# The order of the seven products in the feed-forward stages of a one-core trunk kernel

## The chip, the cores and the metric

The program runs on one core of a Trainium2 chip. The metric is the device time of one execution in microseconds (us); lower is better. Before the change it is 2337.01 us, the median of three runs (2335.78 to 2339.98).

## What is computed

The reference is a two-layer diffusion trunk: 1024 latent tokens of width 1024, and a context of 256 tokens. Each layer normalises and modulates the tokens, mixes them (Fourier and state-space groups in layer 0, gating and pooling groups in layer 1), projects, and adds the result. Then each layer runs the part that matters here, a squared-ReLU feed-forward network of hidden width 4096:

```
lat = lat + g_f * (square(relu(h @ w1)) @ w2)       # h: 1024 x 1024, w1: 1024 x 4096, w2: 4096 x 1024
```

Everything is float32. A float32 product is made on TensorE from a rounded part ("hi") and a remainder ("lo") of both operands, in three matmuls: hi*hi, hi*lo and lo*hi (`mm3`).

## The kernel before

**Seven products in place of eight.** Both halves of the feed-forward network are multiplied by a fast 2x2 block scheme. A product P1 to P7 multiplies one combination of weight blocks with one combination of activation blocks (a *set*). The table `PRODUCTS` (line 259) gives for each product its weight tile, its set, and one of three accumulators in PSUM: `a`, `b` or `d`. P1, P6, P7 and P4 all add onto accumulator `a`, one after another; P5 and P3 share `d`; P2 has `b` to itself. So the running value in `a` must be read out after P1 before P6 may write, after P6 before P7 may write, and after P7 before P4 may write.

**Stages.** `ffn` (line 1535) runs 16 stages per layer, here numbered 0 to 15. Stages 0 to 7 make the hidden activations ("up"), two quads (pairs of column tiles) in each, stages 8 to 15 multiply them by `w2` ("down"), two quads in each except stage 15, which has one. A stage runs its seven products one after another. `product` (line 1521) issues for each quad 4 x 3 = 12 matmuls of 128x128 by 128x512. With two quads a product is 24 matmuls: quad 0, then quad 1. Six PSUM banks (`psg`) serve as accumulators: three per quad.

**Reading the accumulators.** In an up stage (`up_step`, line 1556) P1, P5 and P6 are copied from PSUM by ScalarE (line 1586), P2, P7 and P3 are added to one of these copies by VectorE (line 1588), and P4 goes through a ReLU on ScalarE (line 1590). After P2, P7 and P3 ScalarE also does a ReLU (1595) and a square (1564) over both quads. In a down stage (`down_step`, line 1615) VectorE reads all seven (`add_to`, line 1548): each adds the accumulator times a gain onto a tile of `lat`. The first use of a `lat` tile waits for its load (`need`, line 1609, DMA at line 501).

**Weights.** `Weights` (line 267) loads the blocks, forms the sums s1, s2, s3 (`sum`, line 286) and splits each into hi (ScalarE, line 489) and lo (VectorE, line 490). `split` works in the order in which the products use the weights. s4 = w12 - s2 is formed by VectorE (line 295) right after w12 was split. All weights rotate through 14 tiles, so a split often waits for a product to release a tile.

**Sets.** A finished set of the up stages goes to DRAM (`r_d`, DMA on POOL's queue, line 1561) and is loaded for the down stages one product at a time (`load_set`, line 1551, DMA on SP's queue, line 1476), into the place of a set that has been used for the last time, and is then split (`late`, `split_set`).

**Other work beside.** In layer 0 the feed-forward stages from stage 2 on also carry the modulation vectors of the next layer: `ada_steps` (line 646) loads 256 KB pieces (SP, line 654) and VectorE accumulates them (line 658).

**What sets the order.** Each engine executes its own queue in order. The framework places the instructions of the program into the queues ahead of time, by priority and by its own estimate of when each is ready; a split may stand a product or two earlier than in the program text. The order cannot change at run time. Stage 0 has an order of its own, `FIRST` (line 262: P1, P2, P5, P6, P7, P3, P4), which the change leaves alone; there the first product of stage 1 stands between P1 and P2. All other stages use `ORDER` (line 261).

The loops around the change, cut to their core:

```
for s, p in enumerate(w.order):     # ffn, line 1665
    run(p)                          # the product, its reads, puts or loads of sets
    ...
    w.step(s)                       # splits the weight used three products on
    nxt.step(s - 7)                 # loads, sums and splits for the next stage
```

Of the kernel before, what the change touches and what calls it, by code (L numbers as in the profile page):

```python
# [176 lines left out]
class FfnNorm:  # L177
# [44 lines left out]
    def second(self):  # L222
# [28 lines left out]
        for j in range(2):  # L251
# [6 lines left out]

PRODUCTS = {"p1": ("w11", "b11", "a"), "p2": ("w12", "b21", "b"), "p3": ("s4", "b22", "d"), "p4": ("w22", "t4", "a"),
            "p5": ("s1", "t1", "d"), "p6": ("s2", "t2", "a"), "p7": ("s3", "t3", "a")}  # L260
ORDER = ["p1", "p5", "p6", "p2", "p7", "p3", "p4"]
FIRST = ["p1", "p2", "p5", "p6", "p7", "p3", "p4"]
SETS = ["b11", "t1", "t2", "b21", "t3", "b22", "t4", "b12"]
SETPOOL = {"b11": "C", "t1": "A", "t2": "A", "b21": "A", "b22": "A", "t3": "B", "t4": "B", "b12": "B"}


# [188 lines left out]
class Trunk:  # L455
# [257 lines left out]
    def layer0_mixer(self):  # L713
# [8 lines left out]
        self.col_d = dp.tile([32, 3, L], F32R, name="col_d")  # L722
        self.r_d = dp.tile([4, len(SETS), P, 4 * HALF], F32, name="r_d")
        self.hb_d = dp.tile([2, NCH, P, 512], F32, name="hb_d")
# [774 lines left out]
    def up_weights(self, layer, n):  # L1499
# [3 lines left out]
        def block(q):  # L1503
            return lambda i, j: w[j * 512:(j + 1) * 512, (4 * n + 2 * q + i) * P:(4 * n + 2 * q + i + 1) * P].rearrange(
                "(k p) c -> p k c", p=P)

        return Weights(self, [block(q) for q in range(2)], ORDER if n else FIRST)

# [26 lines left out]
    def ffn(self, layer, norm, extra, after, first, last):  # L1535
# [15 lines left out]
        def load_set(chunk, p):  # L1551
            src = self.r_d[chunk, SETS.index(p)].rearrange("p (k t) -> p k t", t=HALF)
            sets[p] = self.from_scratch(SETPOOL[p], "r", src)
            late.append(sets[p])

        def up_step(n, w, last_pair, start=None):
# [3 lines left out]
            def put(name):  # L1560
                nc.gpsimd.dma_start(self.r_d[chunk, SETS.index(name)][:, q0 * HALF:(q0 + 2) * HALF], self.flat(tmp[name]))

# [52 lines left out]
        def down_step(chunk, quads, w, final):  # L1615
            banks = {}
            hits = {"p1": (0, 0), "p5": (1, 1), "p6": (0, 1), "p2": (0, 0), "p7": (1, 1), "p3": (0, 1), "p4": (1, 0)}

            def run(p):
                i, hf = hits[p]  # L1620
                for n, q in enumerate(quads):
                    ct = 2 * q + i
                    ps = self.product(banks, w, p, n, sets)
                    need(q, hf)
                    add_to(ct, hf, ps)
                    if final and p in ("p2", "p7", "p3", "p4"):
                        for b, (h, sl) in enumerate(after.blocks):
                            if h == hf:
                                after(ct, b, lat[ct][hf][:, sl])
                if chunk < 3 and quads[-1] == 3:  # L1630
                    load_set(chunk + 1, PRODUCTS[p][1])

            return run
# [13 lines left out]
        for chunk in range(4):  # L1647
            for quads in ((0, 1), (2, 3)) if chunk < 3 else ((0, 1), (2,)):
                w = Weights(self, [self.down_block(layer, chunk, q) for q in quads], ORDER)
                stages.append((w, down_step(chunk, quads, w, chunk == 3)))  # L1650
# [296 lines left out]
```

## Time and profile before

| | |
|---|---|
| median of three runs | 2337.01 us |
| the profiled execution | 2340.41 us, of which span 2338.3 us |
| mean granted TensorE clock | 0.995 of full speed |
| matmul (PE) busy | 2287.6 us, 98% of the span |
| VectorE (DVE) busy | 1595.7 us, 68% |
| ScalarE (ACT) busy | 986.1 us, 42% |
| GpSimd (POOL) busy | 178.5 us, 8% |

The rows come from one profiled execution. In the rows PE is TensorE's matmuls, PEld its weight loads, and SPq and POOLq are the DMA queues of SyncE and GpSimd. L1586 is line 1586 of the kernel. The time between the profiled execution's own time and its span, 2.1 us, lies around the first and last instruction. A matmul's duration in the rows is that of a pipelined instruction; the distance between two starts is what it costs.

### The profile page before, as it was taken

To read this page: it belongs to the slowest core of one execution; us is meant where nothing else is said; L and a number is where in the kernel's file an instruction comes from. 1 tells how busy PE (TensorE), PEld (TensorE's weight loads), DVE (VectorE), ACT (ScalarE), POOL (GpSimd) and SP (SyncE) were. 2 spreads that over 40 slices of the span, in tenths; PEclk is the share of its full clock that TensorE was granted. 3 is DMA by queue.
4 is the path that set the end of the run, shared out by engine and by line. 5 is a ranking of instruction groups with operands and counts; after the bars stand their busy time and mean duration, and the time that the engine had idled before them with its cause. 6 is when DMAs were issued, how large, how long until landed. Compare 5 with 4: busy or idle time off the path is not lost. (4 is left out here: it accounts for less than half of the span.)

```text
span 2338.3 us, 27846 instructions
## 1 busy us (share of the span) xinstructions
PE 2287.6 (98%) x10445; PEld 1840.6 (79%) x10445; DVE 1595.7 (68%) x2100; ACT 986.1 (42%) x1385; POOL 178.5 (8%) x303
## 2 busy tenths in 40 slices
PE   7999999999999999999999999999989999999998
PEld 2787777777877888878888887888868888788887
DVE  4777778757378676778877639642496555887785
ACT  3656664443136454633433322231255554543242
POOL 0003002111000101100001000000010101000000
PEclk9999999999999999999999999999999999999999
DMA  8545567648514656763554225752124536754422
GB/s 306 174 127 160 163 218 247 206 158 303 164 50 167 207 199 222 275 234 123 189 173 132 70 72 176 230 202 104 55 98 157 178 126 222 273 189 171 135 88 111
DMA packets 305169, 400.52 MB, mean 171 GB/s; under 512 B 22063, under 2 KB 222379, under 8 KB 297611
## 3 DMA queue, kind: packets, MB, share of 16 engines
q1 hardware_dynamic: 257952, 297.75, 38.8%
q0 software_dynamic: 30656, 91.78, 10.5%
q10 hardware_dynamic: 16427, 9.22, 1.3%
q8 instruction: 82, 1.34, 0.2%
q14 instruction: 52, 0.43, 0.1%
HBM read 282.27 MB, written 116.39 MB: 170 GB/s over the span
## 5 line engine op out<-in xcount | busy, mean ns | idle before, releaser
L478 PE MATMUL psg<-hhi,whi 128*128 128x512 f32 x1088 | 429.0, 395 | 9.7 <-ACT hhi L489 4.6
L478 PE MATMUL psg<-hlo,whi 128*128 128x512 f32 x1088 | 427.3, 393 | 2.9 <-DVE hlo L490 2.9
L478 PE MATMUL psg<-hhi,wlo 128*128 128x512 f32 x1088 | 424.9, 391 | 0.0
L478 PE MATMUL psg<-rhi,whi 128*128 128x512 f32 (+1 forms) x920 | 356.3, 387 | 5.6 <-DVE lat L1548 5.6
L478 PE MATMUL psg<-rlo,whi 128*128 128x512 f32 (+1 forms) x920 | 355.4, 386 | 0.0
L478 PE MATMUL psg<-rhi,wlo 128*128 128x512 f32 (+1 forms) x920 | 355.1, 386 | 0.0
L478 PEld LDWEIGHTS psg<-hhi,whi 128*128 128x128 f32 x1088 | 205.4, 189 | 56.6 <-ACT hhi L489 7.1
L489 ACT CAST whi<-ww 128x1024 fp32r<-128x1024 f32 (+1 forms) x128 | 131.2, 1025 | 278.4 <-DVE wlo L490 229.3
L478 PEld LDWEIGHTS psg<-hlo,whi 128*128 128x128 f32 x1088 | 205.3, 189 | 48.3 <-DVE hlo L490 5.5
L478 PEld LDWEIGHTS psg<-hhi,wlo 128*128 128x128 f32 x1088 | 205.4, 189 | 43.7 <-issue 1.0
L490 DVE TENSOR_TENSOR wlo<-ww,whi 128x1024 fp32r<-128x1024 f32 (+1 forms) x128 | 152.0, 1187 | 99.0 <-PE psg L478 89.5
L1548 DVE SCALAR_TENSOR_TENSOR lat<-psg,ada,lat 128x512 f32<-128x512 f32 (+1 forms) x220 | 162.7, 741 | 72.1 <-PE psg L478 54.4
L478 PEld LDWEIGHTS psg<-rhi,whi 128*128 128x128 f32 x920 | 173.2, 188 | 41.6 <-issue 5.6
L478 PEld LDWEIGHTS psg<-rlo,whi 128*128 128x128 f32 x920 | 173.2, 188 | 34.9 <-issue 0.2
L478 PEld LDWEIGHTS psg<-rhi,wlo 128*128 128x128 f32 x920 | 173.1, 188 | 34.5
L478 PE MATMUL psg<-h,whi 128*128 128x512 f32 (+1 forms) x672 | 196.1, 373 | 4.2 <-DVE h L509 3.4
L489 ACT CAST whi<-ws 128x1024 fp32r<-128x1024 f32 (+1 forms) x96 | 98.1, 1024 | 170.9 <-PE psg L478 89.7
L478 PE MATMUL psg<-yhi,whi 128*128 128x512 f32 x384 | 151.9, 396 | 2.2 <-ACT nss L133 1.8
L478 PE MATMUL psg<-yhi,wlo 128*128 128x512 f32 x384 | 150.3, 392 | 0.0
L478 PE MATMUL psg<-ylo,whi 128*128 128x512 f32 x384 | 149.8, 391 | 0.0
L490 DVE TENSOR_TENSOR wlo<-ws,whi 128x1024 fp32r<-128x1024 f32 (+1 forms) x96 | 113.9, 1186 | 51.5 <-PE psg L478 45.5
L489 ACT CAST rhi<-rlo 128x1024 fp32r<-128x1024 f32 x116 | 116.0, 1049 | 70.9 <-PE psg L478 46.6
(298 smaller groups left out, 3574.8 us busy)
## 6 DMA issues: line engine op xcount, KB each, us to landing
rlo<-r_d SPq DMA_DIRECT2D x58, 1024.0 KB, 6.8
ww<-in_ffn_w_dram SPq DMA_DIRECT2D x190, 256.0 KB, 5.2
r_d<-rt POOLq DMA_DIRECT2D x64, 512.0 KB, 6.5
araw<-in_ada_w_dram SPq DMA_DIRECT2D x56, 512.0 KB, 5.0
r_d<-uc POOLq DMA_DIRECT2D x36, 512.0 KB, 2.9
lat<-lat_d SPq DMA_DIRECT2D x32, 512.0 KB, 9.2
ws<-in_ffn_w_dram SPq DMA_DIRECT2D x62, 256.0 KB, 3.3
wraw<-in_ev_w_in_dram SPq DMA_DIRECT2D x24, 512.0 KB, 6.7
```

The source lines that it names most:

```text
L478: self.nc.tensor.matmul(out, lhsT=lhsT, rhs=rhs, start=start, stop=stop, skip_group_check=onto)
L489: self.nc.scalar.copy(hi, x)
L490: self.nc.vector.tensor_tensor(lo, x, hi.bitcast(F32), ALU.subtract)
L1548: nc.vector.scalar_tensor_tensor(lt, ps, g(ct), lt, ALU.mult, ALU.add)
```

## The change

Two products change places in `ORDER`, and the same two sets in `SETS`:

```diff
-ORDER = ["p1", "p5", "p6", "p2", "p7", "p3", "p4"]
+ORDER = ["p1", "p5", "p2", "p6", "p7", "p3", "p4"]
 FIRST = ["p1", "p2", "p5", "p6", "p7", "p3", "p4"]
-SETS = ["b11", "t1", "t2", "b21", "t3", "b22", "t4", "b12"]
+SETS = ["b11", "t1", "b21", "t2", "t3", "b22", "t4", "b12"]
```

In the 15 stages of each layer that use `ORDER`, P2 now comes third and P6 fourth. With them move: the reads of their accumulators, the split of w12 (now ahead of s2's), the forming of s4, the ReLU, square and put of P2's result, and in the loading stages the loads of the sets b21 (now third) and t2 (now fourth). `SETS` only names the place of each set in `r_d`. The number of instructions of every kind stays the same.

## Rows read from the trace of the kernel before

**Rows 1.** The page's first part: busy time, share of the span, instructions.

```profile
PE 2287.6 (98%) x10445; PEld 1840.6 (79%) x10445; DVE 1595.7 (68%) x2100; ACT 986.1 (42%) x1385; POOL 178.5 (8%) x303
```

**Rows 2.** The waits of PE: engine, waited for, us in total, times, longest.

```profile
PE psg L478 <- DVE lat L1548: 5.6, 3, 3.2
...
PE psg L478 <- ACT uc L1586: 2.0, 2, 1.0
```

**Rows 3.** Timeline, ACT, layer 1 stage 5: start, us, instruction, count, [idle before <-releaser].

```profile
1907.25 0.59 ACT L1586 COPY uc<-psg 128x512 f32<-128x512 f32 x1 [0.56 <-PE psg L478]
1909.97 0.59 ACT L1586 COPY uc<-psg 128x512 f32<-128x512 f32 x1 [2.13 <-PE psg L478]
...
1917.46 1.05 ACT L1595 ACTIVATE uc<-uc 128x1024 f32<-128x1024 f32 x1
1918.55 1.06 ACT L1564 ACTIVATE uc<-uc 128x1024 f32<-128x1024 f32 x1
```

**Rows 4.** Timeline, DVE, the same stage, the read of P2's second quad.

```profile
1916.39 0.68 DVE L1588 TENSOR_TENSOR uc<-psg,uc 128x512 f32<-128x512 f32 x1
```

**Rows 5.** Timeline, ACT, layer 1 stage 0, copies after P6.

```profile
1727.78 1.56 ACT L1586 COPY uc<-psg 128x512 f32<-128x512 f32 x3 [0.77 <-PE psg L478]
```

**Rows 6.** Timeline, PE, layer 1 stage 0, the first matmul of P7.

```profile
1728.42 0.50 PE L478 MATMUL psg<-hhi,whi 128*128 128x512 f32 x1 [1.04 <-ACT uc L1586]
```

**Rows 7.** Timeline, PE, stage 8: first matmuls of P6 (layer 0, then layer 1 twice).

```profile
1006.86 0.77 PE L478 MATMUL psg<-rhi,whi 128*128 128x512 f32 x1 [3.19 <-DVE lat L1548]
...
2020.12 0.47 PE L478 MATMUL psg<-rhi,whi 128*128 128x512 f32 x1 [1.39 <-DVE lat L1548]
...
2024.07 0.50 PE L478 MATMUL psg<-rhi,whi 128*128 128x512 f32 x1 [0.98 <-DVE lat L1548]
```

**Rows 8.** Timeline, DVE, layer 0 stage 8, reads of accumulators.

```profile
1005.96 0.75 DVE L1548 SCALAR_TENSOR_TENSOR lat<-psg,ada,lat 128x512 f32<-128x512 f32 x1 [6.83 <-DMA lat<-lat_d]
...
1013.57 1.40 DVE L1548 SCALAR_TENSOR_TENSOR lat<-psg,ada,lat 128x512 f32<-128x512 f32 x2
...
1017.16 0.74 DVE L1548 SCALAR_TENSOR_TENSOR lat<-psg,ada,lat 128x512 f32<-128x512 f32 x1
...
1020.09 0.74 DVE L1548 SCALAR_TENSOR_TENSOR lat<-psg,ada,lat 128x512 f32<-128x512 f32 x1
```

**Rows 9.** Timeline, DVE, layer 1 stage 8, the seventh read.

```profile
2034.51 0.75 DVE L1548 SCALAR_TENSOR_TENSOR lat<-psg,ada,lat 128x512 f32<-128x512 f32 x1
```

**Rows 10.** Busy time by window: stretch, length, busy (count) per engine, PEclk, DMA, GB/s.

```profile
1006.00:1010.00 4.00, 3.14 (x8) 2.56 (x9) 3.00 (x4) 0.00 (x0) 0.53 (x1) 0.57 1.07 375
```

**Rows 11.** Timeline, DVE, layer 0, stages 2, 4 and 6.

```profile
772.28 1.53 DVE L658 SCALAR_TENSOR_TENSOR aacc<-araw,silu,aacc 128x512 f32<-128x512 f32 x2 [6.37 <-DMA araw<-in_ada_w_dram]
...
781.22 1.21 DVE L490 TENSOR_TENSOR wlo<-ww,whi 128x1024 fp32r<-128x1024 f32 x1
...
857.01 1.22 DVE L490 TENSOR_TENSOR wlo<-ww,whi 128x1024 fp32r<-128x1024 f32 x1
...
935.46 1.22 DVE L490 TENSOR_TENSOR wlo<-ww,whi 128x1024 fp32r<-128x1024 f32 x1
```

**Rows 12.** Timeline, ACT, layer 0 stage 2, the copies of P6.

```profile
778.69 1.06 ACT L1586 COPY uc<-psg 128x512 f32<-128x512 f32 x2
```

**Rows 13.** Timeline, PE, layer 0, first matmul of P7 in stages 2, 4 and 6.

```profile
780.37 0.39 PE L478 MATMUL psg<-hhi,whi 128*128 128x512 f32 x1
...
858.38 0.39 PE L478 MATMUL psg<-hhi,whi 128*128 128x512 f32 x1
...
936.38 0.39 PE L478 MATMUL psg<-hhi,whi 128*128 128x512 f32 x1
```

**Rows 14.** Timeline, DVE, layer 1 stage 7, a split during the third product's end.

```profile
1988.43 1.22 DVE L490 TENSOR_TENSOR wlo<-ww,whi 128x1024 fp32r<-128x1024 f32 x1
```

**Rows 15.** Timeline, PE, layer 1 stage 7, the last matmul of the fourth product.

```profile
1991.14 0.39 PE L478 MATMUL psg<-hhi,wlo 128*128 128x512 f32 x1
```

**Rows 16.** Timeline, DVE, layer 0 stage 15, the read of P6.

```profile
1272.36 0.75 DVE L1548 SCALAR_TENSOR_TENSOR lat<-psg,ada,lat 128x512 f32<-128x512 f32 x1 [0.40 <-PE psg L478]
```

## The prediction

> **What bounds the kernel now.** I read the page first, then the waits of PE, then the feed-forward stages as timelines, one engine at a time. The page shows PE busy for 98% of the span [rows 1], so a change is worth what it adds to or takes from PE's waits. The waits of PE [rows 2] are short, and the two lines that the change can touch are the first matmul of a product waiting for VectorE's or ScalarE's read of the accumulator that it must add onto. Stage by stage, PE waits in stages 0 and 1's start, and at P6 of stage 8; elsewhere in the feed-forward stages the timelines show matmuls without a gap. So there is little to win, and the question is what the new neighbours in accumulator `a` cost.
>
> **The unit.** Two copies of one product's quads lie 2.72 us apart (1909.97 - 1907.25, rows 3), which is 12 matmuls at 0.227 us: one quad of one product. P6 and P7 use the same accumulator. Before, P2's two quads and the other quad of P6 stand between a quad of P6 and the same quad of P7: 3 x 2.72 = 8.2 us for the read. After, only the other quad: 2.72 us (in stage 15, with one quad, nothing). P1 to P6 gets the same 5.4 us more. The change moves 5.4 us of cover from the pair P6-P7 to the pair P1-P6.
>
> Stage 0 has P6 and P7 side by side already, and there it costs: the copies after P6 begin at 1727.78, three in 1.56 us, about 0.5 us each, and P7's first matmul starts at 1728.42, after 1.04 us of waiting for ScalarE [rows 5, 6]. So the price of a late read is seen in this kernel, in us for us.
>
> **Part 1: the steady up stages (nothing).** After P2's second quad ends (T), VectorE reads it until T+1.7, ScalarE does its ReLU and square (1.05 and 1.06 us) until T+4.2, as at 1916.39 to 1919.61 with T near 1915.4 [rows 3, 4]. P6's first quad ends at T+2.7. If its copy stands behind the square it ends at T+4.8, and P7 would begin at T+5.4 in any case. It is hidden, by 0.6 us. If one more cast of 1.05 us stood in front, 0.5 us would show, in nine stages (1, 3 and 5 of layer 0 and 1 to 6 of layer 1; the others follow below): 0 to 5 us. I take 0, since the rows have the split before the ReLU and it is counted already.
>
> **Part 2: stage 15 (+2).** With one quad P7 begins when P6's read is done. That read began when P6 ended and took 0.75 us [rows 16]; with the tail of the last matmul and the signal I estimate 1.0 us in each layer, 2.0 in all (bounds 1.5 and 4, the latter with a 1.2 us split in front).
>
> **Part 3: stage 8 (+8).** Here `lat` comes late: VectorE waits until 1005.96 [rows 8], and PE waits 3.19 us at P6 in layer 0, and 1.39 and 0.98 us in layer 1 [rows 7]. After the first the granted clock is 0.57 over 4 us [rows 10], so about 1.7 us more go at the low level, 1.2 GHz. With P2 third, P6 begins one product later and these waits are gone: a gain of 3.2 + 1.7 and 2.4 us. But VectorE is then working off a backlog without idle time: its fourth and fifth reads are the double row at 1013.57 (P5's second quad and P6's first), the sixth, P6's second quad, ends at 1017.9, and the seventh, P2's first, begins at 1020.09, because splits of weights and sets stand between. After the change the seventh read is that of P6's first quad, and its place in the queue is set ahead, so it ends near 1020.83. P7 in layer 0 began before at 1006.86 + 48 x 0.227 + 1.7 = 1019.4. After, it begins at 1020.9, following a wait of over 6 us, and loses another 1.7 to the clock: +3.2. In layer 1 the seventh read ends at 2035.26 [rows 9]; P7 began before at 2024.07 + 36 x 0.227 = 2032.2. After: 2035.3 + 1.7 - 2032.2 = +4.8. Sum +8.0. Bounds: -7.3 (if P6's reads are placed so early that both waits go for nothing) and +12 (a second slow stretch of the clock in each layer).
>
> **Part 4: layer 0, stages 2, 4 and 6 (+17).** Here VectorE waits for pieces of the modulation weights, 6.37 us in stage 2 [rows 11], and everything behind in its queue is late. Before, the copies of P6 themselves ended at 779.75 [rows 12], nearly 7 us after the first quad; nobody saw it, since P2 stood in between. The new chain is: the weight split at the end of the third product (781.22, 857.01 and 935.46), which moves back by the read of P2's first quad (0.68), the split itself (1.22), the read of P2's second quad (0.68), ReLU (1.06, behind a cast of 1.05 that starts when the split ends, about 0.3 us more) and the copy (0.59), some 4.5 us in all. P6's copy ends near 785.8, 861.5 and 940.0. P7 began at 780.37, 858.38 and 936.38 [rows 13]. Waits of 5.4, 3.2 and 3.6 us, and 1.7 us each for the clock, since each is at least as long as the one in [rows 7]: 17.3. The bounds are 0, if the copy is placed ahead of the split and VectorE's lag doesn't reach ScalarE, and 22, with the square in front of the copy too. I take the chain without the square.
>
> A rule speaks for this chain: the Trainium skill, page "PSUM — Partial Sum Buffer", section "Engine vs sequencer instructions", says that the queues of ScalarE and VectorE are strictly first in, first out. The trace agrees: in [rows 12] copies whose data was there for 6 us start only after what stood ahead. If an engine could pass over a waiting instruction, parts 3 and 4 would fall to nothing. Another rule speaks against the change as such: "Perfetto Trace Analysis", section "Matmuls", wants independent groups to rotate through PSUM banks so that reading one overlaps the next; by it alone only stage 15, with one quad and so no other bank between, would lose, and the sum would be part 2's.
>
> **Part 5: stage 7 of both layers (+3).** The first casts of loaded sets hold up ScalarE. In layer 1 the split at 1988.43 [rows 14] plus the same 4.5 us gives 1992.9; P7 would begin at 1991.14 + 0.23 [rows 15]: +1.6. I take the same for layer 0: 3.2 (0 to 6).
>
> **What else moves.** w12's split comes one step sooner after its load; s4's 1.2 us on VectorE moves with it; the number of tiles held stays the same in each step, since s2's waits where w12's did. P2's put on POOL's queue goes out 5.4 us earlier, P6 has none. In stages 7 to 15 b21 is loaded third and t2 fourth: each still follows the product that used it last, and the third and fourth products free as many places, so SP's queue is passed at the same times. I count all of this as nothing: its cover is the two products between a split and its use. If w12 came late, VectorE and ScalarE would be held by up to a load; that is in the upper bound.
>
> **Sum.** 2.0 + 8.0 + 17.3 + 3.2 = 30.5 us. The profiled execution took 2340.4 (span 2338.3 and 2.1 around it), 3.4 above the median, so 2371 for such an execution and 2337.0 + 30.5 = 2367.5 for the median. I give 2367.
>
> **Rivals.**
> - *Only the waits on the counted reads (A).* The planner places P6's copies ahead of the lagging splits, so parts 4 and 5 vanish, and parts 2 and 3 stay: 2337 + 10 = 2347. For it: the planner orders by its own estimates, which I can't see. Against: it placed the copies in [rows 12] behind a late cast.
> - *Stage 8's waits go and nothing follows (B, faster).* The 3.2 + 1.7 + 2.4 = 7.3 us at P6 go because P1's reads, for which P6 waited until 1006.86, 2020.12 and 2024.07, are in time for a P6 that comes 5.4 us later; if P6's reads sit right after P5's in VectorE's queue, P7 doesn't wait, and stage 15's 2 us remain: 2337 - 5.3 = 2331.7. It decides if the reads of P6 end by about 1014.4 in layer 0. Against: only five reads have begun by then, and P6's would be the seventh and eighth.
> - *All hidden (C).* Parts 2 to 5 cancel or are covered: 2337, within 5 us. For it: the steady up stages show slack everywhere.
> - *The new ORDER doesn't reach the stages:* excluded, all stages but 0 are built from it.
>
> **Chances.** Forecast (over 15 us slower) 0.56, A 0.17, C 0.13, B 0.14. A measurement of this kernel can tell about 0.2%, 4.7 us, from no change. So slower 0.73, same 0.13, faster 0.14. For the forecast alone 2352 to 2380, with part 1's 5 us and the upper bounds of the parts; to hold eight in ten it reaches down over A and most of C, to 2334.
>
> **What would show it.** Right: waits of P7 (not P6) for ScalarE in layer 0's stages 2, 4 and 6, for VectorE at stage 8 and 15; low granted clock right behind; no wait at P6 of stage 8. Wrong: P7 without waits in stages 2, 4 and 6; VectorE's reads of P6 at stage 8 ahead of 1017; new waits at places not named, as for a late w12 or for a set.

## The result, and the profile after

The changed kernel takes 2371.14 us, the median of four runs (2367.88 to 2376.19), beside 2337.02 for the kernel before (2335.78 to 2339.98): 1.0142 times as long, with a 95% interval of 1.0129 to 1.0156. It is slower by 34 us; the prediction said 2367. The profiled execution took 2369.43 us, span 2367.6, which is 29.3 us more than the span of before. The rest of this text explains these 29.3 us.

The first row is the page's first part, the next two are PE's waits (engine, waited for, us in total, times, longest). They answer [rows 1, 2].

```profile
PE 2296.0 (97%) x10445; PEld 1846.0 (78%) x10445; DVE 1595.6 (67%) x2100; ACT 985.2 (42%) x1385; POOL 178.0 (8%) x303
```

```profile
PE psg L478 <- ACT uc L1586: 17.1, 6, 6.0
PE psg L478 <- DVE lat L1548: 11.5, 2, 6.0
```

Each engine has as many instructions as before. The wait for ScalarE's copy has gone from 2.0 to 17.1 us (stage 0, which has the old order, has 2.0 of the one and 2.3 of the other), the wait for VectorE's read in the down stages from 5.6 to 11.5.

**Where it went, by stage.** A stage's length here is the distance in PE's timeline from its first matmul to the first matmul of the next stage. An undisturbed stage is 38.08 us long (39.93 where the matmuls of the modulation vectors stand in it). The table has every stage that differs by more than 0.05 us between the two kernels, and the others that the prediction gave a price:

| stage | before | after | difference | predicted |
|---|---|---|---|---|
| layer 0, 2 | 38.08 | 44.03 | +5.95 | +7.1 (5.4 + 1.7) |
| layer 0, 4 | 38.08 | 47.25 | +9.17 | +4.9 (3.2 + 1.7) |
| layer 0, 6 | 38.08 | 43.51 | +5.43 | +5.3 (3.6 + 1.7) |
| layer 0, 7 | 39.93 | 39.93 | 0.00 | +1.6 |
| layer 0, 8 | 42.89 | 47.28 | +4.39 | +3.2 |
| layer 1, 7 | 38.08 | 39.35 | +1.27 | +1.6 |
| layer 1, 8 | 41.00 | 45.40 | +4.40 | +4.8 |
| both, 15 | 19.04 | 19.09, 19.04 | +0.05 | +2.0 |
| sum | | | +30.7 | +30.5 |

What precedes stage 0 of layer 0 was 1.1 us shorter in this execution, and that makes most of the difference to 29.3.

PE's timeline (start, us, instruction, count, idle before and its releaser) at the first matmul of P7, in stages 2, 4, 6 and 8 of layer 0 and 7 and 8 of layer 1:

```profile
783.53 0.79 PE L478 MATMUL psg<-hhi,whi 128*128 128x512 f32 x1 [4.16 <-ACT uc L1586]
...
869.33 0.80 PE L478 MATMUL psg<-hhi,whi 128*128 128x512 f32 x1 [6.00 <-ACT uc L1586]
...
954.16 0.80 PE L478 MATMUL psg<-hhi,whi 128*128 128x512 f32 x1 [3.66 <-ACT uc L1586]
...
1039.96 0.80 PE L478 MATMUL psg<-rhi,whi 128*128 128x512 f32 x1 [6.02 <-DVE lat L1548]
...
2016.14 0.50 PE L478 MATMUL psg<-hhi,whi 128*128 128x512 f32 x1 [0.97 <-ACT uc L1586]
...
2060.04 0.79 PE L478 MATMUL psg<-rhi,whi 128*128 128x512 f32 x1 [5.52 <-DVE lat L1548]
```

In [rows 13] the same matmuls of stages 2, 4 and 6 had no wait. In stage 8 the waits have moved: those at P6 [rows 7] are gone, and there is one longer wait at P7 in each layer.

**Stage 2 read closely.** First VectorE's timeline, then ScalarE's (they answer [rows 11, 12]):

```profile
773.49 1.41 DVE L658 SCALAR_TENSOR_TENSOR aacc<-araw,silu,aacc 128x512 f32<-128x512 f32 x2 [3.58 <-DMA araw<-in_ada_w_dram]
...
777.75 0.68 DVE L1588 TENSOR_TENSOR uc<-psg,uc 128x512 f32<-128x512 f32 x1
...
780.15 0.68 DVE L1588 TENSOR_TENSOR uc<-psg,uc 128x512 f32<-128x512 f32 x1
780.75 1.21 DVE L490 TENSOR_TENSOR wlo<-ww,whi 128x1024 fp32r<-128x1024 f32 x1
```

```profile
780.86 1.06 ACT L1595 ACTIVATE uc<-uc 128x1024 f32<-128x1024 f32 x1 [3.74 <-DVE uc L1588]
781.95 1.06 ACT L1564 ACTIVATE uc<-uc 128x1024 f32<-128x1024 f32 x1
782.91 0.57 ACT L1586 COPY uc<-psg 128x512 f32<-128x512 f32 x1
```

Read this as one chain. VectorE stands idle for 3.58 us before a piece of modulation weights, and everything behind the piece in its queue is late: a split, two sums, two more pieces, and among them the reads of P2's two quads, the second of which ends at 780.83. ScalarE has been idle for 3.74 us, since the ReLU at the head of its queue needs that read. P6's copy stands behind ReLU and square and starts at 782.91; P7 starts at 783.53. In the steady stages the same operations do no harm. ScalarE's timeline in layer 1 stage 5 (it answers [rows 3]):

```profile
1935.66 1.06 ACT L1595 ACTIVATE uc<-uc 128x1024 f32<-128x1024 f32 x1
1936.63 0.56 ACT L1586 COPY uc<-psg 128x512 f32<-128x512 f32 x1
1937.09 1.06 ACT L1564 ACTIVATE uc<-uc 128x1024 f32<-128x1024 f32 x1
```

VectorE is in time there, the ReLU doesn't wait, and P6's copy stands even before the square. Stage 7 of layer 1 shows a third transfer at the head of a queue, the first loaded set:

```profile
2007.66 1.05 ACT L489 CAST rhi<-rlo 128x1024 fp32r<-128x1024 f32 x1 [4.51 <-DMA rlo<-r_d]
...
2013.46 1.06 ACT L1595 ACTIVATE uc<-uc 128x1024 f32<-128x1024 f32 x1 [2.38 <-DVE uc L1588]
...
2015.53 0.57 ACT L1586 COPY uc<-psg 128x512 f32<-128x512 f32 x1
```

And in stage 8 of layer 0 it is `lat`. In VectorE's timeline the read of P1's first quad waits for it, and the seventh read, that of P6's first quad, ends at 1039.90, just ahead of P7 at 1039.96 (they answer [rows 8]):

```profile
1024.86 0.75 DVE L1548 SCALAR_TENSOR_TENSOR lat<-psg,ada,lat 128x512 f32<-128x512 f32 x1 [6.33 <-DMA lat<-lat_d]
...
1039.16 0.74 DVE L1548 SCALAR_TENSOR_TENSOR lat<-psg,ada,lat 128x512 f32<-128x512 f32 x1
```

**The clock.** Busy time by window, behind three of the waits (columns as in [rows 10]):

```profile
783.50:787.50 4.00, 3.97 (x11) 3.15 (x12) 1.22 (x1) 2.46 (x3) 0.33 (x1) 0.60 0.76 235
869.30:873.30 4.00, 3.97 (x9) 3.15 (x10) 2.15 (x3) 2.46 (x3) 0.33 (x1) 0.50 0.77 217
...
2016.00:2020.00 4.00, 3.86 (x17) 3.20 (x18) 2.91 (x3) 4.00 (x6) 0.44 (x1) 1.00 1.00 371
```

The granted clock fell to 0.50 of full speed, 1.2 GHz, behind the wait of 6.00 us and did not fall behind the one of 0.97. What a stage lost beyond its wait is 1.8, 3.2 and 1.8 us in stages 2, 4 and 6. Stage 7 of layer 1 lost 0.30 us beyond its wait at full speed (1.27 beside 0.97), so all but some 0.3 us of each is the price of the clock.

**Stage 15.** Here `ORDER` puts nothing between P6 and P7, and nothing is lost. VectorE's timeline in layer 0, the reads of P6 and P7 (the first answers [rows 16]), and PE's row of that stretch:

```profile
1298.87 0.75 DVE L1548 SCALAR_TENSOR_TENSOR lat<-psg,ada,lat 128x512 f32<-128x512 f32 x1 [0.17 <-PE psg L478]
...
1302.77 0.75 DVE L1548 SCALAR_TENSOR_TENSOR lat<-psg,ada,lat 128x512 f32<-128x512 f32 x1 [0.69 <-PE psg L478]
```

```profile
1298.00:1303.00 5.00, 5.00 (x23) 4.06 (x22) 2.90 (x5) 1.05 (x1) 0.00 (x0) 1.00 0.73 245
```

PE is busy without a gap. The read of P7 starts 3.90 us after that of P6, which is 17 matmuls at 0.227 us and not the 12 of P7. The queue of the built program tells why. Around the place between P6 and P7 it holds, in this order (`psg_10178` is accumulator `a`, `psg_10196` is `d`):

```
MATMUL psg_10178<-rhi_9777,whi_10192   and 11 more: P6
MATMUL psg_10196<-rhi_9853,whi_10235   and 4 more: P3, first five
MATMUL psg_10178<-rhi_9813,whi_10210   and 11 more: P7
MATMUL psg_10196<-rhi_9853,wlo_10236   and 6 more: P3, the rest
```

The planner has put five of P3's matmuls between P6 and P7: PE's queue is not in the order of `ORDER`. PE's timeline shows the place. A product's matmuls come in threes (`rhi,whi`, `rlo,whi`, `rhi,wlo`); P6's last starts at 1298.44, and the fifth one behind it is followed by a new beginning in place of its `rhi,wlo`, which is P7's first:

```profile
1299.57 0.39 PE L478 MATMUL psg<-rlo,whi 128*128 128x512 f32 x1
1299.80 0.40 PE L478 MATMUL psg<-rhi,whi 128*128 128x512 f32 x1
```

### The profile page after: what moved, and what is told of

Same layout as the page of the kernel before. It is cut to its first block, busy times and chain, and to the rows that moved or that the text cites. A ratio compares the mean times of both kernels' runs of the same rounds, so it can differ in the third digit from the quotient of the medians.

```text
span 2367.6 us, 27873 instructions
## 1 busy us (share of the span) xinstructions
PE 2296.0 (97%) x10445; PEld 1846.0 (78%) x10445; DVE 1595.6 (67%) x2100; ACT 985.2 (42%) x1385; POOL 178.0 (8%) x303
## 5 line engine op out<-in xcount | busy, mean ns | idle before, releaser
L478 PE MATMUL psg<-hhi,whi 128*128 128x512 f32 x1088 | 431.7, 397 | 24.9 <-ACT uc L1586 17.1
L478 PE MATMUL psg<-rhi,whi 128*128 128x512 f32 (+1 forms) x920 | 357.7, 389 | 11.5 <-DVE lat L1548 11.5
```

What stands on the lines that cost most here:

```text
L478: self.nc.tensor.matmul(out, lhsT=lhsT, rhs=rhs, start=start, stop=stop, skip_group_check=onto)
```

## The experiments

The theory: the new order costs only where a late transfer stands at the head of VectorE's or ScalarE's queue (modulation pieces in stages 2, 4 and 6, `lat` in stage 8, the first set in stage 7), because P6's read then comes later than the one quad of other work between P6 and P7. The main rivals: the order of ScalarE's queue is enough by itself; stage 8 inherits its loss from the up stages; two neighbours on one accumulator cost something everywhere.

Stage lengths in us, worked out from PE's timelines in the same way:

| kernel | L0 st. 2 | 4 | 6 | 8 | L1 st. 7 | 8 |
|---|---|---|---|---|---|---|
| after | 44.03 | 47.25 | 43.51 | 47.28 | 39.35 | 45.40 |
| down only | 38.59 | 38.08 | 38.08 | 44.05 | 38.08 | 44.95 |
| up only | 43.37 | 45.30 | 42.00 | 41.84 | 38.63 | 38.84 |
| three stages | 44.11 | 41.71 | 44.49 | 40.19 | 38.08 | 40.21 |
| no piece loads | 38.08 | 38.08 | 38.08 | 45.49 | 40.11 | 45.63 |
| pieces spread | 45.77 | 38.08 | 40.71 | 46.63 | 41.84 | 45.29 |
| after, `lat` earlier | 43.55 | 45.69 | 44.75 | 43.05 | 39.61 | 40.59 |
| before, `lat` earlier | 38.08 | 38.08 | 38.08 | 38.08 | 38.08 | 38.08 |
| square written later | 43.65 | 41.90 | 41.95 | 47.57 | 39.61 | 45.12 |
| square on VectorE | 39.29 | 39.79 | 40.04 | 44.95 | 41.95 | 45.05 |
| after, `lat` earliest | 45.25 | 43.45 | 43.86 | 39.45 | 38.27 | 38.79 |
| both remedies | 39.07 | 38.84 | 39.19 | 41.95 | 39.45 | 38.14 |

**Parts of the change: down stages only, up stages only, three stages only.** Each keeps a second order and picks one by stage; in the first, on the changed kernel:

```diff
+OTHER = ["p1", "p5", "p6", "p2", "p7", "p3", "p4"]
...
-        return Weights(self, [block(q) for q in range(2)], ORDER if n else FIRST)
+        return Weights(self, [block(q) for q in range(2)], OTHER if n else FIRST)
```

The second is the same line on the kernel before, with `OTHER` the new order; the third uses it there only for `layer == 0 and n in (2, 4, 6)`.

> The new order only in the down stages (8 to 15); the up stages keep the order of before. Theory (the cost is local to the stages whose reads are late): layer 0's stages 2, 4, 6 and layer 1's stage 7 go back to the old time and only stage 8 pays, 4.4 us in each layer, so 8.8 us over the kernel before: about 2346 us (2343 to 2349), with a wait for VectorE of some 5 us at P7 of stage 8 in both layers and none at P7 of stages 2, 4 and 6. Rival (stage 8 is late because the up stages end late: the backlog is handed on): with the old order in the up stages, stage 8 costs nothing or gains the 3 to 5 us of the old wait at P6, about 2332 to 2337 us.

> The new order only in the up stages (1 to 7); the down stages keep the order of before. Theory: the complement of the run before: 20.6 us from layer 0's stages 2, 4, 6 and 1.3 us from layer 1's stage 7, about 2359 us (2355 to 2364); stage 8 shows the old wait at P6 (3.2 us in layer 0) and none at P7. The two parts add up to the 29.3 us by which the span grew. Rival (the two parts are not independent, a late stage 7 makes stage 8 late): stage 8 is longer than before too, 2364 us or more.

> The kernel before with the new order only in layer 0's stages 2, 4 and 6; everything else as before. Theory (these are the stages in which VectorE waits for a piece of the modulation weights while the third product runs): nearly the whole of the up stages' loss, 18 to 22 us, about 2357 us. Rival (the loss is spread: stages 2, 4 and 6 only show what stages 1, 3 and 5 hand on): half or less, 2347 us or below.

Measured beside 2338.16 us for the kernel before: down only 2344.75 (ratio 1.0033, interval 1.002 to 1.0045), up only 2356.15 (1.0079, 1.0062 to 1.0097), three stages 2354.86 (1.0084, 1.0059 to 1.0109). The first two lie where the theory had them, the third a little under it. PE's waits of the down-only kernel and of the up-only kernel (their line numbers are one higher):

```profile
PE psg L479 <- DVE lat L1549: 8.2, 2, 4.1
...
PE psg L479 <- ACT uc L1587: 1.3, 2, 1.1
```

```profile
PE psg L479 <- ACT uc L1587: 15.3, 6, 5.5
...
PE psg L479 <- DVE lat L1549: 2.4, 2, 1.9
```

Each half has its own wait: the 2.4 us for `lat` in the second stand at P6, as before the change. Down only has 0.21 us at P7 of stage 2 as well (38.59), so the old order's cover has its limit too. Stage 8 pays with next to no loss in the up stages (44.05 and 44.95 beside 42.89 and 41.00), and in layer 0 its first `lat` is read 13.3 us into the stage, in the changed kernel 12.8: it comes no later behind late up stages. So stage 8 doesn't inherit its loss: that rival falls. The three stages alone bring 16.1 us of the up stages' loss. The sizes are less firm than the places: the same queues gave 20.6 us in stages 2, 4 and 6 of the changed kernel, 16.4 in up only, and 19.8, 18.3 and 13.3 in three kernels below in which these queues stayed as changed (`lat` earlier, `lat` earliest, square written later).

**The modulation pieces not loaded.** On the changed kernel. What is left out: the 48 loads of 256 KB; VectorE accumulates one resident tile of 0.001 in their place, so layer 1 gets other modulation vectors.

```diff
-                nc.sync.dma_start(wt, w[k * P:(k + 1) * P, part * D + q * cols:part * D + (q + 1) * cols])
+                if load:
+                    nc.sync.dma_start(wt, w[k * P:(k + 1) * P, part * D + q * cols:part * D + (q + 1) * cols])
...
+                    nc.gpsimd.memset(fixed[0], 0.001)
+                yield from self.ada_steps(*e, lambda: fixed[0], accs, False)
```

> The changed kernel without the 48 loads of 256 KB of modulation weights during layer 0's feed-forward stages: VectorE does the same accumulations, but from one tile that is filled once with 0.001 (so layer 1's modulation vectors are others than the reference's). Theory (it is VectorE's wait for these pieces that makes it late, and the copy of P6 on ScalarE stands behind what VectorE hasn't split yet): the waits of P7 in layer 0's stages 2, 4 and 6 fall from 4.2, 6.0 and 3.7 us to under 1 us each, so about 20 us less than the changed kernel, 2350 us; stage 8 and stage 7 keep theirs. Rival (not the wait but the order of ScalarE's queue, with the ReLU and square of P2 in front of the copy, or VectorE's work itself): the three waits stay, 2368 to 2374 us.

Measured: 2349.10 us (2346.22 to 2352.10). Stages 2, 4 and 6 are back at 38.08 to the last digit, with the same accumulations on VectorE. PE's waits, and ScalarE's timeline in stage 2:

```profile
PE psg L478 <- DVE lat L1549: 10.2, 2, 5.6
...
PE psg L478 <- ACT uc L1587: 3.0, 3, 1.7
```

```profile
774.89 1.06 ACT L1596 ACTIVATE uc<-uc 128x1024 f32<-128x1024 f32 x1
775.85 0.56 ACT L1587 COPY uc<-psg 128x512 f32<-128x512 f32 x1
776.31 1.06 ACT L1565 ACTIVATE uc<-uc 128x1024 f32<-128x1024 f32 x1
```

So it is the wait for the pieces and not VectorE's work on them. Two things are mixed in: the other transfers no longer share their queue with the pieces, and without the loads the planner also put the copy ahead of the square, as in the steady stages. The second accounts for 1.06 us of each chain at most, and not for the 3.7 to 6.0 us of the waits.

**The pieces spread over more stages.** All work is kept; the pieces skip the steps of the second to fourth product, and stage 8.

```diff
-                if n >= 2:
+                if n >= 2 and n != 8 and s not in (1, 2, 3):
                     next(sums, None)
```

> The changed kernel with all its work, but the modulation pieces are not taken in the steps of the second, third and fourth product of a stage (P5, P2, P6), nor in stage 8; they spread over more stages instead. Theory (what costs is a piece that VectorE waits for just ahead of the split and the read in front of P6's copy): the waits of P7 in layer 0's stages 2, 4 and 6 vanish or fall under 1 us with nothing left out, some 15 to 20 us less than the changed kernel: 2350 to 2355 us. Rival (the pieces do harm wherever they stand, since VectorE has no slack for them beside these products): the wait moves to other stages, 3, 5, 7 or 9, and the time stays within 5 us of 2371.

Measured: 2359.86 us (2358.28 to 2362.77), between theory and rival. Stage 4 is free of the loss, stage 6 loses 2.6 us, stage 2 loses even more, 7.7. VectorE's timeline in stage 2 shows that the planner still put a pair of pieces ahead of the split, and that they were late:

```profile
774.62 1.42 DVE L658 SCALAR_TENSOR_TENSOR aacc<-araw,silu,aacc 128x512 f32<-128x512 f32 x2 [4.29 <-DMA araw<-in_ada_w_dram]
```

It says that where a piece is written does not settle where it is queued. Stage 5 of layer 0 has a new wait of 0.63 us at P7, a little of what the rival expected. The run neither helps nor hurts the theory.

**`lat` loaded earlier.** On the changed kernel and on the kernel before:

```diff
-                if n == nup - 1 and s == 5:
+                if n == nup - 1 and s == 3:
                     need(0, 0)
                     need(1, 0)
```

> The changed kernel with the first two loads of lat tiles for stage 8 issued two products earlier in stage 7. Theory (VectorE's backlog in stage 8 begins with its wait for the first lat tile): the waits of P7 in stage 8, 6.0 and 5.5 us, shrink, stage 8 loses most of the 9.2 and 7.3 us by which it is over 38.08 us, so 8 to 16 us less than the changed kernel: 2355 to 2363 us. Rival (the backlog comes from the splits of weights and sets between the reads): stage 8 stays within 2 us of what it was, 2367 to 2375 us.

> The kernel before (old order) with the same earlier loads of lat tiles: a try at beating both kernels. Theory: the waits for VectorE at P6 of stage 8 (3.2 us in layer 0, 1.4 and 1.0 in layer 1) go, with the slow clock behind them; stage 8 was 4.8 and 2.9 us over 38.08, so 4 to 8 us faster than before: 2330 to 2333 us. Rival (the earlier loads push the weight loads of stage 7 or 8 back by two loads of 512 KB, which turns up as a wait for a split): same or slower, 2335 to 2342 us.

Measured: on the changed kernel 2358.94 us (2356.70 to 2361.67), 12 us less, as the theory had it; PE's wait for VectorE's reads fell from 11.5 to:

```profile
PE psg L478 <- DVE lat L1548: 5.2, 2, 3.1
```

On the kernel before it gave 2334.26 us (12 runs, 2331.48 to 2335.94) beside 2337.06: ratio 0.9984, interval 0.9975 to 0.9993. It beats both kernels, the one before by 2.8 us rather than the 4 to 8 that were expected. In its profile stage 8 is 38.08 us long in both layers, though VectorE still waits for `lat`:

```profile
1002.07 0.75 DVE L1548 SCALAR_TENSOR_TENSOR lat<-psg,ada,lat 128x512 f32<-128x512 f32 x1 [3.56 <-DMA lat<-lat_d]
```

This is the old order's cover at work: 3.56 us of lateness at a queue's head cost PE nothing. Stage 8's loss before the change varied (42.89 in the profile of before, 40.19 in the three-stages kernel with the same code there), so on average there was less to win than the one profile showed.

**P2's square written later.** On the changed kernel, in stages 1 to 7: P2's ReLU, square and put are held until P6's copies have been written.

```diff
+                if n and p == "p2":
+                    held.append((name, t))
+                elif n and p == "p6":
+                    for name, t in held:
+                        nc.scalar.activation(t, t, AF.Relu)
+                        square(name, t)
...
```

> The changed kernel with P2's ReLU, square and put written after P6's copies (stages 1 to 7), so that the square can stand behind the first copy in ScalarE's queue. Theory (most of the delay of P6's copy comes from VectorE, the square adds its 1.06 us): each of layer 0's stages 2, 4 and 6 where the square does move behind the copy is shorter by 1 to 2 us, the others stay; 0 to 6 us less in all, 2363 to 2372. Rival (P2's ReLU and square in front of the copy are the whole delay): these stages lose their waits, about 2350 us.

Measured: one run, 2362.25 us. Inconclusive: ScalarE's timeline in stage 2 has ReLU, square and copy in the old order, and stages 4 and 6 as well; the planner had moved nothing where it mattered.

```profile
781.91 1.06 ACT L1564 ACTIVATE uc<-uc 128x1024 f32<-128x1024 f32 x1
782.88 0.57 ACT L1588 COPY uc<-psg 128x512 f32<-128x512 f32 x1
```

What is shorter in stages 4 and 6 (41.90 and 41.95) comes from the same queues with other arrivals of the pieces, and from a clock that stayed at full speed (last section).

**P2's square on VectorE.** On the changed kernel: in stages 2, 4 and 6 of layer 0 one VectorE instruction makes ReLU and square, max(t, 0) times t, so that nothing of P2's stands ahead of P6's copy in ScalarE's queue.

```diff
+                    if layer == 0 and n in (2, 4, 6) and p == "p2":
+                        nc.vector.scalar_tensor_tensor(t, t, 0.0, t, ALU.max, ALU.mult)
+                        tmp[name] = t
+                        put(name)
...
```

> The changed kernel, in which in layer 0's stages 2, 4 and 6 VectorE makes P2's ReLU and square in one instruction of max and multiply over both quads, so that ScalarE's queue has no ReLU between the cast and P6's copy. The modulation loads stay. Theory (two things are needed for the loss: VectorE is late by a piece, and a ReLU that needs VectorE stands ahead of the copy in ScalarE's queue; either one gone is enough): the copies follow the cast, 4 to 5 us sooner, the waits of P7 in the three stages vanish, 15 to 20 us less than the changed kernel: 2350 to 2356 us. Rival (the copy would be late in any case, since the cast ahead of it waits for VectorE too, and VectorE gets 1.2 us more to do): waits of 3 to 6 us stay, 2366 to 2375 us.

Measured: 2355.77 us (2352.42 to 2356.95), 15 us less than the changed kernel. ScalarE's and PE's timelines in stage 2:

```profile
776.96 0.59 ACT L1586 COPY uc<-psg 128x512 f32<-128x512 f32 x1 [0.23 <-PE psg L478]
781.68 1.05 ACT L489 CAST whi<-ww 128x1024 fp32r<-128x1024 f32 x1 [4.14 <-DVE wlo L490]
782.64 0.58 ACT L1586 COPY uc<-psg 128x512 f32<-128x512 f32 x1
```

```profile
783.27 0.50 PE L478 MATMUL psg<-hhi,whi 128*128 128x512 f32 x1 [0.91 <-ACT uc L1586]
```

VectorE is as late as ever (its read of P2's second quad ends near 780.5 here), and P6's first copy no longer cares: it starts at 776.96, right behind P6. A smaller wait of 0.91 to 1.65 us is left at P7's second quad, whose copy stands behind a cast that VectorE holds up. So the loss of these stages needs both: a late VectorE, and an instruction that needs it standing ahead of the copy. The edit also cost something elsewhere: stages 5 and 7 of layer 0 are 40.96 and 41.10 us long here, beside 39.93, with waits of 0.73 and 1.05 us at P7 for ScalarE's copy. In stage 5 VectorE waits 3.85 us for a weight load for which it didn't wait in the changed kernel.

**`lat` earliest, and both remedies.** The first has all four loads of `lat` for stage 8 in stage 7's second to fourth steps (below as the second kernel writes it); the second adds to it the square on VectorE, in stages 2, 4 and 6 of layer 0 and in stage 7 of both layers.

```diff
-                if n == nup - 1 and s == 5:
+                if n == nup - 1 and s == 1:
                     need(0, 0)
                     need(1, 0)
-                if n == nup and s < 2:
-                    need(s, 1)
+                if n == nup - 1 and s in (2, 3):
+                    need(s - 2, 1)
```

> The changed kernel with the first four loads of lat tiles placed in stage 7's second to fourth steps, ahead of most loads of sets there. Theory (all of stage 8's loss begins with lat tiles that come late; with the first load two products earlier VectorE still waited 1.8 and 3.4 us for them in layer 0): stage 8 falls to within 1 us of 38.08 in both layers, 16 us less than the changed kernel, about 2353 to 2358 us. Rival (what is left comes from the splits of weights and sets in front of P6's read, or the sets are now late in turn): stage 8 stays 2 us or more above 38.08, or stage 7 and later stages get new waits; 2358 to 2370 us.

> The changed kernel with both remedies: the four early loads of lat tiles, and P2's ReLU and square on VectorE in layer 0's stages 2, 4 and 6 and in stage 7 of both layers. Nothing is left out. Theory (the three places were the whole loss, and the new order costs nothing once none of the three queues is held up by a late transfer): all of 29.3 us comes back, and what stage 8 lost before the change too, 5 to 8 us: 2331 to 2337 us, level with the old order with earlier loads of lat tiles (2334.3), not better than it. Rival (the order with two neighbours on one accumulator costs something in itself, in whatever stage is least covered): 2340 us or more.

Measured: `lat` earliest, one run, 2351.22 us, a little under the theory; stage 8 is 39.45 and 38.79, so 1.4 and 0.7 us over an undisturbed one, where the changed kernel was 9.2 and 7.3 over. PE's wait:

```profile
PE psg L478 <- DVE lat L1548: 1.5, 2, 1.1
```

Nearly all of stage 8's loss began with `lat`. The rest did not: VectorE waits for no `lat` here, and the seventh read still ends 22.9 and 22.2 us into the stage, where P7 is due at 21.8. Both remedies: 2341.25 us (11 runs, 2338.89 to 2343.77) beside 2337.96, ratio 1.0018, interval 1.0009 to 1.0027. The theory's 2337 was missed and the rival's bound of 2340 holds: with the worst transfers dealt with, the new order still costs 3 to 4 us against the kernel before, and 7 against the old order with `lat` earlier. PE's waits show that it is the same places, now small:

```profile
PE psg L478 <- ACT uc L1586: 4.4, 7, 1.0
...
PE psg L478 <- DVE lat L1548: 2.0, 1, 2.0
```

The largest is stage 8 of layer 0 (41.95, a wait of 2.02 us and the slow clock behind it). ScalarE's timeline at the end of stage 7, and VectorE's at the seventh read:

```profile
990.68 1.05 ACT L489 CAST whi<-ww 128x1024 fp32r<-128x1024 f32 x1 [2.30 <-DMA ww<-in_ffn_w_dram]
```

```profile
1019.35 0.74 DVE L1548 SCALAR_TENSOR_TENSOR lat<-psg,ada,lat 128x512 f32<-128x512 f32 x1
```

VectorE waits for no `lat`. It is held up by this cast of a weight that comes late, until 991.76, and from there to the end of the seventh read, at 1020.09, its timeline shows no idle time: it works off its own queue, splits of loaded sets above all. So late transfers are not the whole cost. In stage 8 the new order leaves VectorE next to no room even without them. Whether the earlier loads of `lat` made the weight late was not tried.

## Why the prediction was right, and where it was not

**The mechanism: right.** The change moved 5.4 us of cover from P6-P7 to P1-P6; the losses sit at P7 and the waits at P6 of stage 8 went. The stage terms add up to 30.7 us where the prediction had 30.5, but that agreement is luck: parts 2 and 5 were some 1.9 us too high each, part 3 was 0.8 and part 4 3.3 too low.

**Part 1 (steady up stages, nothing): right.** These stages differ by 0.04 us at most.

**Part 2 (stage 15, +2.0): wrong; measured 0.05.** The step that failed is "with one quad P7 begins when P6's read is done". It took the program's order for PE's. The planner filled the gap with five matmuls of P3, 1.13 us, which is just what the estimate of 1.0 us needed. The page "Perfetto Trace Analysis" of the Trainium skill (section "Matmuls"), by which independent groups should rotate through banks, would have let only this stage lose. The trace shows the reverse: nothing was lost here, and 30 us where another bank stood between.

**Part 3 (stage 8, +8.0): right; measured 8.8.** The old waits went and nothing was gained by it, as predicted, since the seventh read in VectorE's queue became P6's. It ended 27.9 us into the stage in layer 0, where the prediction had 28.2. Layer 0 was 4.4 rather than 3.2, as the stage lost 3.2 us beyond its wait and not 1.7; layer 1 was 4.4 rather than 4.8. Taking `lat` forward removed nearly all of it.

**Part 4 (stages 2, 4 and 6, +17.3): right in place and in the kind of chain, too small; measured 20.6.** Two links of the chain were wrong, and nearly cancel. The square, 1.06 us, does stand ahead of the copy (the prediction took the chain without it and kept it for the bound of 22). The split of 1.22 us that the prediction counted ahead of P2's second read stands behind it, in stage 2 at 780.75. Two terms were too small. Beyond the waits went 1.8, 3.2 and 1.8 us, 6.7 in all beside 5.1, since the low level of the clock lasted longer behind the wait of 6.00 us. And the waits themselves, 4.16, 6.00 and 3.66, add up to 13.8 beside 12.2, though the first two were 1.2 too long and 2.8 too short: the rows of before fix when a piece came in that one execution, and the runs above show that this varies.

The strict order of the queues, for which the prediction named the page "PSUM — Partial Sum Buffer" (section "Engine vs sequencer instructions") of the Trainium skill, was tested: with the ReLU out of ScalarE's queue, P6's copy in stage 2 came 5.95 us sooner (776.96 beside 782.91) while VectorE stayed late.

**Part 5 (stage 7, +1.6 in each layer): half right; 1.27 in layer 1, 0.00 in layer 0.** Taking layer 0 from layer 1 was the step that failed. ScalarE's and PE's timelines of the changed kernel in layer 0 show what covers it:

```profile
993.28 0.57 ACT L1586 COPY uc<-psg 128x512 f32<-128x512 f32 x1
```

```profile
993.86 1.84 PE L478 MATMUL psm<-cmat,aacc 128*128 128x1 f32 x16
```

The cast of the first loaded set started 13.3 us into the stage there (14.4 in layer 1), and P6's copy ended 21.75 us into it, just when P7 was due. And the extra matmuls that make the stage 39.93 us long stand exactly between P6 and P7, so that P7's first matmul starts only at 995.56. By these times either would have been enough.

**The rivals.** A (only the reads that were counted) needed P6's copies ahead of the lagging splits; they were behind. B needed P6's reads by 1014.4 in layer 0's stage 8; the read that P7 waited for ended at 1039.90, in a stage that began 19 us later than before. C fell with the waits.

The predicted 2367 is 4 us under the median of 2371.14. The profiled execution, 2369.43, is nearer to the 2371 that the prediction gave for one like that of before. An agreement within 2 to 4 us is no test of the terms, since the same queues gave 13.3 to 20.6 us for part 4 alone. The executions themselves spread too: the four of the changed kernel over 8.3 us, the kernel before over 10 in 17 later ones, and the old order with `lat` earlier, which has no wait in stage 8, over 4.5 in 12. That fits waits that depend on arrivals; it was not tested.

## What to carry to other kernels

The cover between two products that share an accumulator must be measured against the worst lateness of the queue that reads it, with the transfers that may stand at its head, and not against the time of the read: 2.7 us were enough in every steady stage and 1 to 6 us short where a transfer was late. Where such a wait shows, look for the instruction at the head of the reader's queue and what it waits for; loading that earlier (`lat`, two products) or taking the dependent instruction out of the queue (P2's ReLU) brought back 12 and 15 us here, and the first of these made the old order faster too. Neither makes a thin cover safe: with both, the new order still lost 3 to 4 us, in part behind another load and VectorE's own work. An order written in the program is not the order of the queue: look there before a gap, or a remedy, is priced.

## What the runs showed of the hardware

**The clock after a wait.** The length of PE's wait did not settle whether the granted clock fell. Windows behind three waits, of 3.57 us (`lat` earliest, stage 4 of layer 0), of 3.52 us (square written later, the same stage) and of 1.90 us (up only, stage 8 of layer 0). PE had run without a gap from the stage's start up to each:

```profile
867.87:871.87 4.00, 4.00 (x11) 3.22 (x12) 2.11 (x3) 2.42 (x3) 0.30 (x1) 0.60 0.78 222
```

```profile
866.69:870.69 4.00, 4.00 (x18) 3.30 (x19) 2.11 (x3) 2.43 (x3) 0.30 (x1) 1.00 0.78 220
```

```profile
1021.30:1025.30 4.00, 4.00 (x11) 3.15 (x12) 3.82 (x4) 0.86 (x1) 0.53 (x1) 0.57 0.98 375
```

The first two waits are alike to 0.05 us: one is followed by the low level, 1.2 GHz, for most of the window, the other by full speed, 2.4 GHz. The third is little more than half as long, and the low level follows it. A price for the clock per wait is therefore an average.

**Repeatable to the digit.** In all 13 profiles stages 2 to 6 of layer 1 and 9 to 14 of both layers are 38.08 us long within 0.01 (but for two of the kernel with spread pieces, where the modulation matmuls went). In such a stage a difference of a tenth of a microsecond can be read from a single profile, where the whole kernel needs ten runs to tell 3 us. In a stage with a wait it can't: stage 2 of layer 0 took 43.37 to 45.77 us with the same queues.
